# A place of its own for each row sum: the vector engine's scratch for row two moved into a freed transfer buffer

## Chip, cores, metric

One Trainium2 chip, one core. The time is microseconds (us) on the device for one launch, lower is better. The median of the kernel before is 82.82 us (82.77 to 82.85, 3 runs). Engines in short: PE (matmul), DVE (vector), ACT (scalar), POOL (GpSimd), SP (queues of transfers and the end).

## The reference, cut

```python
batch, num_classes = 256, 32000          # logits float32, 32.77 MB
log_probs = logits - max;  log_probs -= log(sum(exp(log_probs)))
smooth_targets = smoothing / num_classes everywhere, plus 1 - smoothing at the label
return -sum(smooth_targets * log_probs, axis=-1)      # one loss per row
```

Each logit is needed twice, in a sum of the logits and in a sum of their exps. The rest is work on one number per row.

## The kernel before, the parts that matter

128 partitions hold two rows each. A row is loaded in pieces; each piece goes to DVE (sum of the logits, by adding its two halves and accumulating) and to ACT (sum of exps). The pieces of row two get smaller so that little is left to do after the last has landed. The elementwise result of a sum is not needed, only its accumulator; it goes into a scratch, `jd`.

```python
WIDTHS = (
    (8000, 12480, 11520),
    (8576, 6400, 4608, 3392, 2496, 1856, 1408, 1088, 832, 704, 640),
)
FOLLOW = (1, 2, 6)   # row two's first 1 + 2 + 6 pieces reuse the three buffers wide0, wide1, wide2
# ... the last two pieces have buffers of their own (tail)

    def sum_logits(xt, w: int, out: bass.AP):
        h = w // 2
        jd = junk.tile([P, max(WIDTHS[0]) // 2], FP32, name="jd", tag="jd")   # bufs=1: one scratch
        return nc.vector.scalar_tensor_tensor(
            out=jd[:, :h], in0=xt[:, :h], scalar=1.0, in1=xt[:, h:w],
            op0=ALU.mult, op1=ALU.add, accum_out=out,
        )
# ...
    for t, w in enumerate(WIDTHS[r]):            # row two
        left = last - t
        xt = load(w, col)
        col += w
        part = sum_logits(
            xt, w, xsum[:, t + 1 : t + 2] if left > 1 else pairs[1 - left][:, 0:1]
        )
        # ... exps = sum_exps(...) on ACT; small additions on DVE when left <= 3
        elif left < 2:
            i = 1 - left
            nc.vector.tensor_tensor(out=done[i + 1][:], in0=done[i][:], in1=pairs[i][:], op=ALU.add)
# ... ln, two transposes, res, one store
```

As every sum writes the same scratch, a sum gets a wait for the sum ahead of it (a *self wait*: DVE waits on DVE), beside the wait for its transfer, unless an instruction between them has waited for that sum already. In the built program such a second wait stands in an instruction of its own ahead of the sum, which does nothing but wait (a *queue instruction*; DVEq in the chain).

The softmax here doesn't subtract the row's maximum and nothing guards it: scores larger than these inputs give would overflow.

## Time and profile before

| | before |
|---|---|
| median | 82.82 us |
| span of the profiled execution | 81.7 us |
| busy: DVE, ACT | 37.0 us (45%), 58.0 us (71%) |
| read from HBM (the chip's main memory) | 32.77 MB at 401 GB/s over the span |
| chain that ended last | transfers 81%, ACT 13%, DVE 2% |

The span is the time from the first to the last instruction in the profile. A transfer *lands* when its last byte has arrived. The chain is followed back from the last instruction, at each step to what released it. An engine's busy share says how much room it has; the chain and the waits say whether anything waits for it. The lines are in the prediction.

### The profile page before, as it was taken

The numbers are of one execution on the slowest core, as the hardware profiler recorded it, in microseconds if no ns is written. First come the engines' busy times: TensorE is split into PE (matmuls) and PEld (weight loads), VectorE is DVE, ScalarE is ACT, GpSimd is POOL, SyncE is SP. The second block draws the span as 40 slices with busy tenths as digits, with TensorE's granted clock in tenths as the row PEclk, the third lists the DMA queues.
The fourth block names the chain that finished last, engine by engine and source line by source line (L and its number), as shares of the span: only waits on it lengthen the run. The fifth ranks groups of instructions, "written<-read, shape, count | busy, mean of one in ns | idle before, by whom it ended". The sixth has DMA issues, their size and how long they took to land.

```text
span 81.7 us, 215 instructions
## 1 busy us (share of the span) xinstructions
PE 6.5 (8%) x21; PEld 4.6 (6%) x21; DVE 37.0 (45%) x37; ACT 58.0 (71%) x31; POOL 10.1 (12%) x19
## 2 busy tenths in 40 slices
PE   0000000000000000000000000000100000399302
PEld 0000000000000000000000000000000000378100
DVE  0000001990000899300299702990295748467772
ACT  5000001999200899993299998999999999999990
POOL 3201640040100000000000002991000000000000
PEclk9999999999999999999999999999999999999997
DMA  6999999999998888998699699999999999999910
GB/s 140 391 463 385 478 541 391 391 391 416 684 440 385 361 361 361 677 406 361 269 538 504 302 538 389 414 401 401 433 424 398 425 448 420 418 426 407 410 59 1
DMA packets 2258, 32.77 MB, mean 401 GB/s; under 512 B 337, under 2 KB 338, under 8 KB 1106
## 3 DMA queue, kind: packets, MB, share of 16 engines
q1 hardware_dynamic: 2018, 30.71, 88.6%
q10 hardware_dynamic: 144, 2.06, 5.9%
q0 software_dynamic: 96, 0.00, 0.1%
HBM read 32.77 MB, written 0.00 MB: 401 GB/s over the span
## 4 chain that ended last, share of the span: by engine, by line
DMA 81%; ACT 13%; DVE 2%; issue 1%; PE 0%; DVEq 0%
DMA wide<-in_logits_dram 57%; DMA tail<-in_logits_dram 24%; ACT ja L326 13%; DVE jd L311 1%; DVE done L421 0%; DVE lin_row L440 0%; PE lin_t L333 0%; DVE res L442 0%; DVEq L421 0%; DVEq L442 0%
## 5 line engine op out<-in xcount | busy, mean ns | idle before, releaser
L326 ACT ACTIVATE ja<-wide 128x8000 bf16<-128x8000 f32 (+4 forms) x5 | 40.2, 8033 | 20.8 <-DMA wide<-in_logits_dram 20.8
L311 DVE SCALAR_TENSOR_TENSOR jd<-wide 128x4000 f32<-128x4000 f32 (+11 forms) x12 | 34.5, 2876 | 39.0 <-DMA wide<-in_logits_dram 39.0
L326 ACT ACTIVATE jt<-wide 128x4608 bf16<-128x4608 f32 (+6 forms) x7 | 14.2, 2068 | 0.1
L428 PE MATMUL warm<-wide,ident 128*128 128x256 f32 x18 | 5.6, 479 | 12.0 <-DMA wide<-in_logits_dram 12.0
L428 PEld LDWEIGHTS warm<-wide,ident 128*128 128x128 f32 x18 | 4.4, 250 | 13.1 <-DMA wide<-in_logits_dram 12.3
L333 PE MATMUL loss_t<-ident,loss 128*1 128x128 f32 x1 | 0.4, 373 | 58.4 <-POOL loss L369 58.4
L358 POOL TENSOR_TENSOR lin<-acc,weighted 128x1 f32<-128x1 f32 x1 | 4.5, 4484 | 0.1
L333 PEld LDWEIGHTS loss_t<-ident,loss 128*1 128x1 f32 x1 | 0.1, 79 | 58.4 <-POOL loss L369 58.4
L353 POOL TENSOR_TENSOR acc<-sums 128x2 f32<-128x2 f32 x1 | 0.2, 192 | 16.2 <-ACT ja L326 16.2
L244 POOL DMA_INDIRECT gat<-in_logits_dram,flat_idx x2 | 2.0, 993 | 0.7 <-POOL ident masks.py:199 0.4
L372 DVE COPY res<-loss_t 1x128 f32<-1x128 f32 x1 | 0.3, 280 | 3.7 <-PE loss_t L333 3.7
L211 ACT ACT_TABLE_LOAD x1 | 1.3, 1283 | 0.9 <-PEq L469 0.9
L353 POOL TENSOR_TENSOR acc<-acc,sums 128x2 f32<-128x2 f32 x1 | 0.2, 193 | 12.6 <-ACT ja L326 12.6
L270 POOL TENSOR_SCALAR weighted<-gat 128x1 f32<-128x1 f32 x1 | 0.9, 867 | 6.4 <-DMA gat<-in_logits_dram,flat_idx 6.4
L326 ACT ACTIVATE jt<-tail 128x704 bf16<-128x704 f32 (+1 forms) x2 | 1.5, 764 | 0.0
L326 ACT ACTIVATION_READ_ACCUMULATOR jt<-wide 128x1 f32 x7 | 1.2, 166 | 0.0
L311 DVE SCALAR_TENSOR_TENSOR jd<-tail 128x352 f32<-128x352 f32 (+1 forms) x2 | 1.0, 510 | 0.1
L311 DVE DVE_READ_ACCUMULATOR jd<-wide 128x1 f32 x12 | 1.0, 82 | 0.0
L224 POOL DMA_DIRECT2D lab<-in_labels_dram x1 | 0.8, 766 | 1.0 <-POOLq L469 1.0
L326 ACT ACTIVATION_READ_ACCUMULATOR ja<-wide 128x1 f32 x5 | 0.9, 173 | 0.0
L236 POOL TENSOR_TENSOR flat_idx<-rowoff,lab 128x2 int32<-128x2 int32 x1 | 0.2, 193 | 5.3 <-DMA lab<-in_labels_dram 5.3
L270 POOL TENSOR_SCALAR xsum<-gat 128x1 f32<-128x1 f32 x1 | 0.2, 208 | 2.9 <-DMA gat<-in_logits_dram,flat_idx 2.9
(24 smaller groups left out, 4.7 us busy)
## 6 DMA issues: line engine op xcount, KB each, us to landing
wide<-in_logits_dram SPq DMA_DIRECT2D x1, 6240.0 KB, 25.9
wide<-in_logits_dram SPq DMA_DIRECT2D x1, 5760.0 KB, 39.1
wide<-in_logits_dram SPq DMA_DIRECT2D x1, 4288.0 KB, 29.6
wide<-in_logits_dram SPq DMA_DIRECT2D x1, 3200.0 KB, 20.5
wide<-in_logits_dram SPq DMA_DIRECT2D x1, 2304.0 KB, 25.8
wide<-in_logits_dram ACTq DMA_DIRECT2D x1, 2016.0 KB, 13.7
wide<-in_logits_dram SPq DMA_DIRECT2D x1, 1984.0 KB, 11.4
wide<-in_logits_dram SPq DMA_DIRECT2D x1, 1696.0 KB
```

The source lines that it names most:

```text
L211: nc.scalar.add_instruction(mybir.InstLoadActFuncSet(name=nc.get_next_instruction_name(), act_func_set_id=tbl, ins=[], outs=[],))
L224: nc.gpsimd.dma_start(out=lab[:], in_=labels.bitcast(I32).rearrange("(p f) -> p f", p=P))
L236: nc.gpsimd.tensor_tensor(out=flat_idx[:], in0=rowoff[:], in1=lab[:].rearrange("p (r two) -> p r two", two=2)[:, :, 0:1], op=ALU.add,)
L244: nc.gpsimd.indirect_dma_start(out=gat[:, r : r + 1], out_offset=None, in_=logits[:], in_offset=bass.IndirectOffsetOnAxis(ap=flat_idx[:, r ...
L270: nc.gpsimd.tensor_scalar(out=weighted[r], in0=gat[:, r : r + 1], scalar1=label_weight, scalar2=None, op0=ALU.mult,)
L311: return nc.vector.scalar_tensor_tensor(out=jd[:, :h], in0=xt[:, :h], scalar=1.0, in1=xt[:, h:w], op0=ALU.mult, op1=ALU.add, accum_out=out,)
L326: return nc.scalar.activation(out=ja[:, :w], in_=xt[:, :w], func=AF.Exp, accum_out=out)
L333: nc.tensor.transpose(out=row[:], in_=column, identity=ident[:])
L353: nc.gpsimd.tensor_tensor(out=acc[:], in0=total, in1=sums[:, :, t : t + 1], op=ALU.add)
L358: nc.gpsimd.tensor_tensor(out=lin[:], in0=total[:, 0, :], in1=weighted[0], op=ALU.add)
L372: nc.vector.tensor_copy(out=res[:, :, 0:1], in_=loss_t[:])
L428: nc.tensor.matmul(warm[:], lhsT=ident[:], rhs=xt[:, i * WARM_COLS : (i + 1) * WARM_COLS], start=True, stop=True,)
```

## The change

Intent: from the third piece of row two on (4608 columns), each sum gets a stretch of scratch of its own, so that no sum has to wait for the one ahead. That needs (4608 + 3392 + ... + 640) / 2 = 8512 columns, more than `jd` has. They are found in `wide0`, the buffer of row two's first piece, which no later load uses.

```diff
-    def sum_logits(xt, w: int, out: bass.AP):
+    SPARE_FROM = 2
+    spare_width = max(WIDTHS[0][0], WIDTHS[1][0])
+    spare = []
+    def sum_logits(xt, w: int, out: bass.AP, place: int | None = None):
         h = w // 2
-        jd = junk.tile([P, max(WIDTHS[0]) // 2], FP32, name="jd", tag="jd")
+        if place is None:
+            jd = junk.tile([P, max(WIDTHS[0]) // 2], FP32, name="jd", tag="jd")[:, :h]
+        else:
+            if not spare:
+                spare.append(wide.tile([P, spare_width], FP32, name="spare", tag="wide0"))
+            jd = spare[0][:, place : place + h]
         return nc.vector.scalar_tensor_tensor(
-            out=jd[:, :h],
+            out=jd,
# ... in row two's loop:
-            xt, w, xsum[:, t + 1 : t + 2] if left > 1 else pairs[1 - left][:, 0:1]
+            xt, w, xsum[:, t + 1 : t + 2] if left > 1 else pairs[1 - left][:, 0:1],
+            sum(WIDTHS[r][SPARE_FROM:t]) // 2 if t >= SPARE_FROM else None,
```

Seen in the built programs: the order of instructions is the same on all engines; six sums (3392 to 832 columns) lose their self wait; that of 4608 columns waits for ACT (end of the exp of the first piece) where it waited for DVE; the last two had no self wait before either, as the small additions ahead of them had already waited for it.

More of the change, by code (lines that the diff above doesn't have):

```diff
@@ L306, in load @@
         return xt
-    def sum_logits(xt, w: int, out: bass.AP):
-        h = w // 2
-        jd = junk.tile([P, max(WIDTHS[0]) // 2], FP32, name="jd", tag="jd")
+    SPARE_FROM = 2
+    spare_width = max(WIDTHS[0][0], WIDTHS[1][0])
+    assert FOLLOW[0] == 1 and sum(WIDTHS[1][SPARE_FROM:]) <= 2 * spare_width
+    spare = []
+    def sum_logits(xt, w: int, out: bass.AP, place: int | None = None):
+        h = w // 2
+        if place is None:
+            jd = junk.tile([P, max(WIDTHS[0]) // 2], FP32, name="jd", tag="jd")[:, :h]
+        else:
+            if not spare:
+                spare.append(
+                    wide.tile([P, spare_width], FP32, name="spare", tag="wide0")
+                )
+            jd = spare[0][:, place : place + h]
         return nc.vector.scalar_tensor_tensor(
-            out=jd[:, :h],
+            out=jd,
             in0=xt[:, :h],
@@ L390 @@
         part = sum_logits(
-            xt, w, xsum[:, t + 1 : t + 2] if left > 1 else pairs[1 - left][:, 0:1]
+            xt,
+            w,
+            xsum[:, t + 1 : t + 2] if left > 1 else pairs[1 - left][:, 0:1],
+            sum(WIDTHS[r][SPARE_FROM:t]) // 2 if t >= SPARE_FROM else None,
         )
```

## The prediction

> **What bounds the kernel now.** I read the page first (busy shares, then the chain that ended last), then the table of stages, then the instructions in order of time for the last 20 us, and last the waits. The chain:
>
> ```profile
> span 81.7 us, 215 instructions
> PE 6.5 (8%) x21; PEld 4.6 (6%) x21; DVE 37.0 (45%) x37; ACT 58.0 (71%) x31; POOL 10.1 (12%) x19
> DMA 81%; ACT 13%; DVE 2%; issue 1%; PE 0%; DVEq 0%
> HBM read 32.77 MB, written 0.00 MB: 401 GB/s over the span
> ```
>
> The reader is to see that the span is a transfer: 81% of the chain is the landing of logits, and the vector engine (DVE), which the change touches, holds 2%. Being busy 45% of the time says only that DVE has room. The 13% of ACT is one exp of the first row that holds a buffer which a later transfer needs; the change doesn't touch it. The stages of row two, from its first sum on (columns: stretch, its length, busy time and count of PE, PEld, DVE, ACT, POOL, then granted clock, DMA share, GB/s):
>
> ```profile
> 58.00:64.00 6.00, 0.37 (x1) 0.08 (x1) 3.93 (x4) 5.84 (x3) 0.19 (x1) 1.00 1.03 439
> 64.00:70.00 6.00, 0.00 (x0) 0.00 (x0) 4.26 (x4) 6.00 (x3) 0.00 (x0) 1.00 0.98 418
> 70.00:78.00 8.00, 5.59 (x18) 4.39 (x18) 5.23 (x15) 8.00 (x13) 0.00 (x0) 1.00 0.99 409
> 78.00:81.70 3.70, 0.54 (x2) 0.16 (x2) 1.82 (x8) 1.80 (x6) 0.00 (x0) 0.84 0.01 3
> ```
>
> Up to 78 us the DMA engines are full (0.98 to 1.03) and ACT is full too (6.00 of 6.00, 8.00 of 8.00), while DVE works 5.23 of 8. The widths were chosen so that each exp ends as the next piece lands. After 78 us nothing is transferred, and what remains is a serial end of 3.7 us. The changed sums, in order of time (start, duration, engine, what; in brackets the idle time before it and what ended it):
>
> ```profile
> 63.76 2.56 DVE L311 SCALAR_TENSOR_TENSOR jd<-wide 128x2304 f32<-128x2304 f32 x1 [1.27 <-DMA wide<-in_logits_dram]
> 67.76 1.93 DVE L311 SCALAR_TENSOR_TENSOR jd<-wide 128x1696 f32<-128x1696 f32 x1 [1.44 <-DMA wide<-in_logits_dram]
> ...
> 75.99 0.73 DVE L311 SCALAR_TENSOR_TENSOR jd<-wide 128x544 f32<-128x544 f32 x1 [0.39 <-DMA wide<-in_logits_dram]
> 77.00 0.59 DVE L311 SCALAR_TENSOR_TENSOR jd<-wide 128x416 f32<-128x416 f32 x1 [0.21 <-DMA wide<-in_logits_dram]
> ...
> 77.92 0.53 DVE L311 SCALAR_TENSOR_TENSOR jd<-tail 128x352 f32<-128x352 f32 x1
> 78.56 0.16 DVE L421 TENSOR_TENSOR done<-done,pair 128x2 f32<-128x2 f32 x1
> 78.71 0.49 DVE L311 SCALAR_TENSOR_TENSOR jd<-tail 128x320 f32<-128x320 f32 x1
> 79.32 0.16 DVE L421 TENSOR_TENSOR done<-done,pair 128x2 f32<-128x2 f32 x1
> ```
>
> Seven of the nine sums that move begin out of idleness, and what ends the idleness is always a piece landing. In all (columns: who waited for whom, us in total, times, longest):
>
> ```profile
> DVE jd L311 <- DMA wide<-in_logits_dram: 5.7, 7, 1.4
> ```
>
> The seven idle times are 1.27, 1.44, 1.04, 0.81, 0.56, 0.39 and 0.21 us, sum 5.7. No wait of a sum for an earlier sum shows in the view of waits at all.
>
> **What the Trainium skill says.** (1) "Perfetto Trace Analysis", Identifying Dependency Chains: an instruction that waits on several engines may get separate semaphore instructions ahead of it. The trace agrees: the chain has queue steps of DVE (DVEq, 0.02 us each) ahead of the small additions of line 421, which wait on DVE and ACT. The kernel sorts the waits so that the transfer's is taken by the sum itself. (2) "VectorE: DVE Perf Modes", The DRAIN you can't avoid: eight copies took the same 13.88 us with a semaphore behind each and with one behind the last. The trace agrees in part: the copy of line 404 begins at 76.64, within the sum that ends at 76.72; but where an addition must wait for a result, the chain has 0.09 us (0.03 issue, 0.02 DVEq, 0.04 issue) between them. (3) Same page, Two Vector instructions with no wait between them: a next instruction that is not held may start before the earlier one has finished. That is what freeing the sums from each other could in principle win; it needs two sums that stand back to back, and the trace shows none among those that lose a wait. (4) "SBUF — State Buffer", Who interferes with whom: transfers and engines use different ports, so a write of DVE into a transfer buffer should cost no more than one into other scratch. The trace agrees: see the fit below.
>
> **The change, part by part.** The order of instructions on all engines is the same before and after, with the same shapes: 14 sums, 14 exps, 15 loads. Only the waits of DVE differ.
>
> *Removed:* six sums (pieces of 3392, 2496, 1856, 1408, 1088 and 832 columns) wait for the earlier sum, since all write the same scratch, and for their transfer; afterwards they wait for the transfer alone. The wait taken away was over by the time of the transfer in each: the previous sum had ended 0.21 to 1.44 us earlier, except that the copy of line 404 stands between the last two. So each saves 0 on the path. If, against the trace, each cost its whole 0.09 us, the sum would be 6 x 0.09 = 0.54 us, 0.65% of 82.82: even the ceiling lies within 2%.
>
> *Replaced:* the sum of the 4608 piece waited for the previous sum (ended 62.49). It now waits for ACT's exp of the first piece of row two, the last reader of the buffer taken over. That exp and its accumulator read end at 57.75 + 0.15 = 57.90, the sum starts at 63.76: 5.86 us of slack. Cost 0.
>
> *Not changed:* the sums of the two last pieces (704 and 640) waited for their transfer alone before, and do so after; the additions of line 421 keep their waits. And these are the ones that set the end: the 704 piece lands at 77.90 and DVE goes on 0.02 later; then 0.55 + 0.09 + 0.16 + 0.50 + 0.10 + 0.17 us up to 79.49, then the transposes, the store. Nothing there loses a wait.
>
> *Buffers and transfers:* the scratch lies in the first transfer buffer after its second and last use. No load waits for it; the loads' waits are the same list. The first scratch keeps its size, so no address moves.
>
> *Duration of a sum:* from 128x320 in 0.494 us and 128x6240 in 6.657 us the slope is 6.163 / 5920 = 1.041 ns per element, the constant 0.161 us. The 128x2304 between them should then take 2.560, and took 2.559, with the DMA engines full. So no contention is there to be relieved, and I expect the same durations in the new place.
>
> Sum: 0 on the path; I allow 0.03 us for small shifts in the queue. 82.82 - 0.03 = 82.79, I say 82.8.
>
> **Rivals.**
> 1. *The self waits do cost.* If the engine's queue is slow to pick up a sum behind its separate wait, the sums start later after a landing than they could. Against it: DVE and ACT are released by the same landings and start together (63.76 and 63.76, 70.73 and 70.75), so DVE isn't the late one; and only the 832 piece's sum is close enough to the end to matter, since DVE is done with its batch (lines 410 and 407) at 77.87, 0.03 before the 704 piece lands. An earlier sum would then wait for that landing. At most 0.54 us: 82.3.
> 2. *A new wait on ACT.* ACT is the fuller engine, and the sum of 4608 now waits for it. For a cost, ACT would have to be 5.86 us later than now. If it were a wrong wait, for an exp later than that of the first piece, DVE would be tied to ACT, each sum behind an exp, perhaps 1 us more at the end: 83.8. The list of waits shows one wait only, on the sum of 4608.
> 3. *Writes into a transfer buffer meet the transfers.* In the last 15 us the transfers go into the neighbouring buffers at full rate. If a sum took 5% longer there, the two on the end's path would add 0.05 x (0.53 + 0.49) = 0.05 us: 82.9. If the batch before got longer than its 0.03 us of slack, some hundredths more.
> 4. *The time is the transfer's, and varies with it.* The profiled execution took 83.03 us, the median of three is 82.82. A difference of 0.2 us can come from the transfers alone, and would hide anything said above.
>
> **Range and chances.** The path gives 82.8. Rivals 1 and 3 move it by +0.1 or -0.3 in plausible sizes, and rival 4 by 0.2 either way, so 82.5 to 83.1 should hold 8 times in 10. Faster by 2% needs 81.2 us, three times the ceiling of rival 1; slower by 2% needs 84.5, which only rival 2 in a strong form comes near. Chances: 0.02 faster, 0.96 within 2%, 0.02 slower.
>
> **What would show it.** In the changed kernel's profile: the nine sums write the new scratch with durations within 0.02 us of those above; seven of them still begin out of idleness ended by a landing, total about 5.7 us; no wait on ACT for the 4608 sum; the chain from 77.9 us on has the same members and durations; DMA still some 81% of the chain and 401 GB/s. I am wrong if the sums' idle time falls while their starts move up against the exps released by the same landing (rival 1), if a wait of a sum on ACT appears (rival 2), if the sums lengthen (rival 3), or if the time after the last landing changes by more than 0.1 us. If only landings shift, with all else the same, it is rival 4.

## The result and the profile after

After: 82.87 us median (82.75 to 83.17, 6 runs), before in the same rounds 82.81 (82.74 to 83.17, 6 runs). Ratio 1.0004, 95% interval 0.9981 to 1.0027: the same. A ratio here is the mean time of one kernel's fast runs over that of the other's of the same rounds, so not quite the ratio of the medians; in the experiments below it fits the listed runs only if the first, profiled execution is left out.

From the page and the waits of the changed kernel: the span and the number of instructions, then who waited for whom (total us, times, longest).

```profile
span 81.6 us, 209 instructions
...
DVE spare L325 <- DMA wide<-in_logits_dram: 5.4, 7, 1.4
```

There were 215 instructions before: the six that are missing are the separate queue instructions that carried the six self waits. So the change did what it was to do. But the nine sums in the new place still begin, seven times, only when a piece lands, and idle 5.4 us for it (5.7 before). The same sums in order of time:

```profile
63.65 2.56 DVE L325 SCALAR_TENSOR_TENSOR spare<-wide 128x2304 f32<-128x2304 f32 x1 [1.02 <-DMA wide<-in_logits_dram]
...
67.66 1.93 DVE L325 SCALAR_TENSOR_TENSOR spare<-wide 128x1696 f32<-128x1696 f32 x1 [1.44 <-DMA wide<-in_logits_dram]
...
75.87 0.73 DVE L325 SCALAR_TENSOR_TENSOR spare<-wide 128x544 f32<-128x544 f32 x1 [0.38 <-DMA wide<-in_logits_dram]
...
76.89 0.59 DVE L325 SCALAR_TENSOR_TENSOR spare<-wide 128x416 f32<-128x416 f32 x1 [0.21 <-DMA wide<-in_logits_dram]
...
77.80 0.53 DVE L325 SCALAR_TENSOR_TENSOR spare<-tail 128x352 f32<-128x352 f32 x1
...
78.58 0.49 DVE L325 SCALAR_TENSOR_TENSOR spare<-tail 128x320 f32<-128x320 f32 x1
```

Durations are those of before to 0.01 us and idle times to 0.02 us, but for the first idle time (1.02 for 1.27). There the sum ahead ended 0.14 us later (62.63 for 62.49) and the piece of 4608 landed 0.11 us earlier. That is not the change: two kernels below that keep this sum's self wait (each sum twice, waits kept; written over the piece before) show 1.03 and 1.01 us there. From the start of the 352-element sum to that of the last DVE instruction (`res`) it is 77.80 to 80.09 = 2.29 us, before 77.92 to 80.22 = 2.30. The pieces landed 0.1 us earlier in this execution, and the sums and the end moved with them, no more.

One view looks quite different, the chain's shares by engine; here of the changed kernel:

```profile
DMA 57%; ACT 23%; issue 16%; PE 0%; DVE 0%
```

Before it was DMA 81%, ACT 13%. The change did not cause this: the same changed kernel, profiled once more (first experiment), has the old chain again.

```profile
DMA 81%; ACT 13%; DVE 2%; issue 1%; PE 0%; DVEq 0%
```

The reason stands at the end. The last DVE instruction waits for two things, DVE's own copy `lin_row` and PE's transpose `lse_t` of ACT's result. In the changed kernel's timeline:

```profile
79.71 0.28 DVE L457 COPY lin_row<-lin_t 1x128 f32<-1x128 f32 x1 [0.36 <-PE lin_t L347]
...
79.78 0.27 PE L347 MATMUL lse_t<-ident,lse 128*1 128x128 f32 x1
80.09 0.28 DVE L459 SCALAR_TENSOR_TENSOR res<-lin_row,lse_t 1x128 f32<-1x128 f32 x1
```

They end at 79.99 and 80.05. From the end of `lin_row` to `res` the chain of before has 0.09 us (0.03 issue, 0.02 DVEq, 0.04 issue), from the end of `lse_t` that of the changed kernel has 0.04, so the two sides reach `res` within some 0.01 us of each other. In before they do as well: `lin_row` ends at 80.12, `lse_t` at 80.16, and `res` starts at 80.22. Whichever side is later by a hundredth decides whether the chain is followed back through DVE to the last landing, or through ACT's row of exps, which in turn keep pace with the landings. The page splits a tie at its end into two very different pies.

### The profile page after: what moved, and what is told of

Read it like the earlier page. It is cut to its first block, busy times and chain, and to the rows that moved or that the text cites. A ratio compares the mean times of both kernels' runs of the same rounds, so it can differ in the third digit from the quotient of the medians.

```text
span 81.6 us, 209 instructions
## 1 busy us (share of the span) xinstructions
PE 7.7 (9%) x21; PEld 5.4 (7%) x21; DVE 37.0 (45%) x37; ACT 57.8 (71%) x31; POOL 10.2 (12%) x19
## 4 chain that ended last, share of the span: by engine, by line
DMA 57%; ACT 23%; issue 16%; PE 0%; DVE 0%
DMA wide<-in_logits_dram 57%; ACT ja L340 20%; ACT jt L340 3%; PE lse_t L347 0%; DVE res L459 0%; ACT lse L454 0%
## 5 line engine op out<-in xcount | busy, mean ns | idle before, releaser
L325 DVE SCALAR_TENSOR_TENSOR jd<-wide 128x4000 f32<-128x4000 f32 (+4 forms) x5 | 25.2, 5047 | 33.5 <-DMA wide<-in_logits_dram 33.5
L325 DVE SCALAR_TENSOR_TENSOR spare<-wide 128x2304 f32<-128x2304 f32 (+6 forms) x7 | 9.3, 1326 | 5.4 <-DMA wide<-in_logits_dram 5.4
L445 PE MATMUL warm<-wide,ident 128*128 128x256 f32 x18 | 6.8, 560 | 11.7 <-DMA wide<-in_logits_dram 11.7
L445 PEld LDWEIGHTS warm<-wide,ident 128*128 128x128 f32 x18 | 5.2, 295 | 13.2 <-DMA wide<-in_logits_dram 12.0
L325 DVE SCALAR_TENSOR_TENSOR spare<-tail 128x352 f32<-128x352 f32 (+1 forms) x2 | 1.0, 508 | 0.0
L325 DVE DVE_READ_ACCUMULATOR spare<-wide 128x1 f32 x7 | 0.6, 83 | 0.0
```

Of the source, the lines that this page charges most:

```text
L325: return nc.vector.scalar_tensor_tensor(out=jd, in0=xt[:, :h], scalar=1.0, in1=xt[:, h:w], op0=ALU.mult, op1=ALU.add, accum_out=out,)
L445: nc.tensor.matmul(warm[:], lhsT=ident[:], rhs=xt[:, i * WARM_COLS : (i + 1) * WARM_COLS], start=True, stop=True,)
```

## The experiments

My theory: a self wait is over before the landing that releases the sum, so taking it away wins nothing, and nothing on DVE before the 704 piece has landed can win anything. Rivals: (a) the two halves of the change cancel, a gain from the waits and a loss from the new place; (b) the sums do hold something back, and the change only failed to free it; (c) self waits cost nothing anywhere. Each experiment's times are beside runs of the kernel before on the same chip; the first four shared one chip (before 82.78 us median, 11 runs), the next three another (82.81, 9 runs), the last three ran together, on the chip of the first four. Their runs of before (82.77, 12 runs) are the 11 of the first four, some 12 minutes older, and one more.

**The changed kernel again.**

> The changed kernel once more, on the chip of the next three, so that small differences have a common yardstick. Theory (the waits taken away were over before the landing that released each sum): ratio to before 1.000, within 0.003. Rival 'the waits cost and the new place costs as much, so they cancel here': the same here; the next two runs tell them apart.

82.80 us, ratio 1.0000 (0.9987 to 1.0012). With this the difference is known to be under 0.15 us either way.

**Own places, but inside the old scratch** (one half of the change):

```diff
-    SPARE_FROM = 2
-    spare_width = max(WIDTHS[0][0], WIDTHS[1][0])
+    SPARE_FROM = 3
+    spare_width = max(WIDTHS[0]) // 2
-                    wide.tile([P, spare_width], FP32, name="spare", tag="wide0")
+                    junk.tile([P, spare_width], FP32, name="spare", tag="jd")
```

> A place of its own for each sum from the piece of 3392 on, but inside the old scratch: five self waits fewer, nothing written into a transfer buffer. Theory: ratio to before within 0.003 of 1, sums' idle times and durations as before. Rival 'cancelling': waits cost about 0.09 us each, so this half alone gains 0.3 to 0.5 us, ratio 0.994 to 0.996.

82.82 us, ratio 1.0006 (0.9994 to 1.0018); 210 instructions, so five waits fewer. No gain from the waits alone.

**The freed buffer, but one place** (the other half):

```diff
-            sum(WIDTHS[r][SPARE_FROM:t]) // 2 if t >= SPARE_FROM else None,
+            0 if t >= SPARE_FROM else None,
```

> The scratch in the freed transfer buffer, but one place for all sums, so the six self waits stay: the other half alone. Theory: ratio within 0.003 of 1 and durations of the nine sums within 0.02 us of before (0.49 to 2.56). Rival 'cancelling': this half alone loses 0.3 to 0.5 us, ratio 1.004 to 1.006, and its sums are longer.

82.91 us, ratio 1.0006 (0.9993 to 1.0020; with the profiled execution of 83.28 us it would be 1.0015); 215 instructions; the nine sums take 0.49 to 2.56 us as before. No loss of the size that the rival asked for (1.004 to 1.006). Rival (a) is out: there is nothing to cancel.

**No middle sums at all** (a wrong result; those sums enter the loss with a factor of 0.1/32000):

```diff
+    nc.gpsimd.memset(xsum[:], 0.0)
-        part = sum_logits(xt, w, ...)
+        if t < 2 or left < 2:
+            part = sum_logits(xt, w, ...)
```

> Wrong result on purpose: the kernel before without the seven sums of the pieces 4608 to 832, with xsum set to zero in their place. It takes away all that the change touches, but for the two last sums. Theory (the landings set the pace up to 77.9 us): ratio 1.000 within 0.003. Rival 'the sums hold something back (engine, memory or transfers), and the change failed to free it': a gain, 0.5 us or more.

82.82 us, ratio 1.0004 (0.9992 to 1.0016). Seven sums with 9.3 us of busy time are gone, and the time is the same. This is the strongest bound: whatever one does to these seven sums, nothing can be won beyond the noise (0.07 us, by the interval). The timeline shows why: DVE now idles until the 704 piece lands, and starts its sum at 77.89 (77.92 before), in both 0.02 us after the landing.

```profile
77.89 0.53 DVE L312 SCALAR_TENSOR_TENSOR jd<-tail 128x352 f32<-128x352 f32 x1 [0.52 <-DMA tail<-in_logits_dram]
```

Rival (b) is out. Do self waits cost anything, then? For that DVE has to be the late one.

**Each sum twice, waits kept** (before's kernel; from the piece of 3392 on, the second result in a spare column):

```diff
+        if t >= 3:
+            part = sum_logits(xt, w, extra[:, t : t + 1])
```

> The kernel before with each sum from the piece of 3392 on done twice (the second into a spare column), all in the one scratch: 16 sums back to back, each waiting for the one ahead, so DVE falls behind the landings and sets the end. Both theories: slower than before. Worked out from before's durations: 2 x 7.75 us of sums, 16 gaps of 0.09, 0.5 for the additions between, from 67.8 us on: DVE ends at 85.2 in place of 79.5, time about 88.5 us.

**Each sum twice, all in places of their own** (changed kernel with SPARE_FROM = 3, and the second sums in `jd` at the same offsets):

```diff
+            if second and not again:
+                again.append(junk.tile([P, max(WIDTHS[0]) // 2], FP32, name="again", tag="jd"))
+            jd = (again if second else spare)[0][:, place : place + h]
```

> The same 16 sums, but each in a place of its own (first ones in the freed buffer, second ones in the old scratch): one self wait left among the sums. My theory (a self wait costs where sums stand back to back: 0.09 us of gap and about 0.08 us of overlap lost, and nothing where a landing comes later): about 86.4 us, some 2 us under the waiting one, and sums start before the one ahead ends. Rival 'a self wait costs nothing even back to back[...]': within 0.3 us of the waiting one.

87.93 us with waits (ratio 1.0617, 1.0600 to 1.0634), 85.91 without (1.0375, 1.0360 to 1.0391): 2.02 us apart, where I had said some 2. Both came 0.5 us under my figures. In the waiting one the sums began at 67.66 and not 67.8, and from there to the end of the last addition (84.37) the gaps and additions came to 1.26 us beside 15.45 of sums, where I had allowed 1.94; the end after it took 3.56 us, not 3.3. The built programs differ by 12 waits of DVE on itself (16 on sums, against one on a sum, one on the reduction and two on additions). The two sums of 928 elements and the sum that follows, with waits:

```profile
74.73 1.12 DVE L311 SCALAR_TENSOR_TENSOR jd<-wide 128x928 f32<-128x928 f32 x1
75.78 0.08 DVE L311 DVE_READ_ACCUMULATOR jd<-wide 128x1 f32 x1
75.90 1.12 DVE L311 SCALAR_TENSOR_TENSOR jd<-wide 128x928 f32<-128x928 f32 x1
76.95 0.08 DVE L311 DVE_READ_ACCUMULATOR jd<-wide 128x1 f32 x1
77.14 0.89 DVE L311 SCALAR_TENSOR_TENSOR jd<-wide 128x704 f32<-128x704 f32 x1
```

and without:

```profile
74.11 1.12 DVE L329 SCALAR_TENSOR_TENSOR spare<-wide 128x928 f32<-128x928 f32 x1
75.15 0.08 DVE L329 DVE_READ_ACCUMULATOR spare<-wide 128x1 f32 x1
75.15 1.12 DVE L329 SCALAR_TENSOR_TENSOR again<-wide 128x928 f32<-128x928 f32 x1
76.20 0.09 DVE L329 DVE_READ_ACCUMULATOR again<-wide 128x1 f32 x1
76.20 0.89 DVE L329 SCALAR_TENSOR_TENSOR spare<-wide 128x704 f32<-128x704 f32 x1
```

Start to start, the first pair takes 75.90 - 74.73 = 1.17 us with the wait and 1.04 without: the wait costs 0.13. To the next sum, which waits for a transfer as well, it is 1.24 against 1.05: 0.19. There the self wait stands in a queue instruction of its own; though the piece had landed long before (the exp of that piece ran from 74.6), the extra instruction costs. Over the pieces 3392 to 1408 the two costs are 0.11 to 0.13 and 0.19 to 0.20. Without a wait the next sum starts together with the accumulator read of the one ahead, 0.08 to 0.09 us before that ends. One thing else differs in the built programs: where nobody waits for them, 9 of the 16 sums don't signal their end any more. It is not what counts, as the last sums (of 832, 704 and 640 columns) signal in both and overlap just the same without a wait (the two of 352 elements start 0.44 us apart, at a duration of 0.52). Rival (c) is out: the change takes away a real cost, from a place where nobody pays it.

**A wait that is not hidden.** The kernel before, with the sums from 3392 on (1856 excepted, because PE still reads the piece before it) written over the piece before, so that each waits for ACT's exp of that piece (*tied* to it, below):

```diff
-    def sum_logits(xt, w: int, out: bass.AP):
+    def sum_logits(xt, w: int, out: bass.AP, into=None):
+        jd = into
+        if into is None:
+            jd = junk.tile(...)
# in row two's loop, with before = xt of the previous turn:
+            before if t >= 3 and left != WARM_LEFT - 1 else None,
```

> The kernel before, but the sums from the piece of 3392 on (that of 1856 excepted) are written over the piece before, so each waits for ACT's exp of that piece, which ends as late as the landing or later. A wait that is not hidden. Theory: at the end the sum of 704 columns starts at the end of the exp of 832 (78.08 + 0.05) and not at 77.92, that of 640 at 78.84 + 0.05 and not at 78.71: +0.2 us, ratio 1.002 to 1.003. Rival 'only landings and their spread count, what DVE waits for changes nothing visible': the traces' sums start as before and the end after the last landing is as long.

83.44 us, ratio 1.0078 (1.0065 to 1.0092): 0.65 us, three times what I had said. The spans, 81.74 on average against 81.49 before, give 0.25 us, the size that the theory has, though not by its way: in the trace the sum of 704 starts at 78.10, behind the reduction ahead of it (77.92 to 78.08), while the exp's accumulator read was over at 78.00. The late sum of 832 had pushed the reduction. The sums' durations are as before (0.49 to 1.93), so it is the waits that cost, not the place. The other 0.4 us lies outside the span of the profile: time minus span is 1.73 us on average, against 1.32 for before, and 1.31 to 1.36 for each of the six experiments above. Three more runs were to place that.

**The same again, then its halves.** Only the last two sums tied (`before if left < 2`), and only the middle ones (`before if t >= 3 and left >= 2 and left != WARM_LEFT - 1`):

> The same kernel as the one written over the piece before, which cost 0.65 us where I had said 0.2: its spans were 0.25 us longer, as said, but the time outside the span was 1.7 us in place of 1.3. Is that outside part the kernel's? If it is an accident of that chip or session, this run has 1.3 us outside and a ratio of 1.003; if the kernel's, 1.7 us and 1.008 again.

> Only the two last sums (704 and 640 columns) are written over the piece before and wait for ACT's exp. In the span: the sum of 704 starts about 0.25 us after its landing in place of 0.02, the span is 0.15 to 0.25 us longer. Outside the span: 1.7 us if what costs there comes from these two, 1.3 if from the middle ones.

> Only the sums of 3392 to 832 columns (that of 1856 excepted) are tied to the exp before, the two last are as before. In the span: the sum of 832 starts about 0.25 us after its landing, so DVE ends the small additions after the 704 piece has landed and not 0.03 us before: 0.15 to 0.2 us longer. Outside: 1.7 us if the middle ones cost there, 1.3 if not.

| | time | ratio (95%) | mean span, longer than before by | time minus span |
|---|---|---|---|---|
| before | 82.77 | | (its span: 81.47) | 1.33 |
| all tied, again | 83.46 | 1.0086 (1.0071 to 1.0101) | 0.28 | 1.73 |
| last two tied | 83.00 | 1.0025 (1.0010 to 1.0039) | 0.21 | 1.33 |
| middle ones tied | 83.32 | 1.0067 (1.0051 to 1.0084) | 0.16 | 1.72 |

Spans are on record to 0.1 us each, so the differences of their means are good to some hundredths only. Inside the span the theory's sizes hold: 0.21 us for the last two (said 0.15 to 0.25), 0.16 for the middle ones (said 0.15 to 0.2). The last two tied is the clean case, as nothing is lost outside. Its timeline:

```profile
77.69 0.21 ACT L328 ACTIVATION_READ_ACCUMULATOR jt<-wide 128x1 f32 x1
77.79 0.79 ACT L328 ACTIVATE jt<-tail 128x704 bf16<-128x704 f32 x1
78.00 0.52 DVE L313 SCALAR_TENSOR_TENSOR wide<-tail 128x352 f32<-128x352 f32 x1 [0.32 <-ACT jt L328]
...
80.21 0.28 DVE L446 SCALAR_TENSOR_TENSOR res<-lin_row,lse_t 1x128 f32<-1x128 f32 x1
```

and of before:

```profile
77.96 0.79 ACT L326 ACTIVATE jt<-tail 128x704 bf16<-128x704 f32 x1
...
80.22 0.28 DVE L442 SCALAR_TENSOR_TENSOR res<-lin_row,lse_t 1x128 f32<-1x128 f32 x1
```

DVE was free at 77.68 and waits for ACT's accumulator read, which ends at 77.90; before, it waited for nothing but the landing. From the start of ACT's exp of that piece (77.79 here, 77.96 before) to `res` (80.21, before 80.22) it is 2.42 us for 2.26. So a wait costs something here from the last two sums on, or where it eats the 0.03 us of slack ahead of them (the middle ones).

The 0.4 us outside the span belongs to the kernel with the middle sums tied, three times out of three (1.73, 1.73 and 1.72), on two chips, while the last two tied, run in the same rounds, had 1.33. What it is stays open: the profile's first and last instructions are as before, and the built programs' opening and closing instructions are the same. It doesn't touch the change studied here, which had 1.30 us outside.

No version beat both kernels, and with the middle sums worth nothing there was none to try among them.

## Why the prediction was right

82.8 us was said, 82.87 measured, inside 82.5 to 83.1, and the ratio says no change. By its steps:

- *Six self waits removed, 0 on the path.* Right: 215 to 209 instructions, idle times before the sums unchanged but for the first (explained above), and the waits alone (own places in the old scratch, five of the six) gave 1.0006.
- *One wait replaced by one on ACT, 0.* Right: in the list of waits of the profile no sum waits for ACT.
- *Same durations in the new place.* Right, to 0.01 us, and shown by itself (freed buffer, one place: 1.0006).
- *The end is not touched.* Right: 2.29 us for 2.30.
- *The ceiling of 0.54 us if each wait cost 0.09 in full.* Too low. The 0.09 counted the gap behind an addition that must wait. The overlap lost and the extra queue instruction come on top: 0.19 us each, measured back to back, so 6 x 0.19 = 1.1 us, 1.4% of the time. The conclusion (within 2% even then) stood, with less room than I claimed. Reading (2) of the skill was too kind, too: that the copy of line 404 starts within the sum ahead speaks against a semaphore that costs nothing, and the sums done twice showed the cost.
- *Rival 1*, that self waits slow the pick-up behind a landing: refuted here, though they do cost where sums queue. *Rival 2*, a wait on ACT: refuted, and its size known now: had the sums really been tied to the exps, it would have been 0.25 us inside the span and 0.65 to 0.7 us in all, the rest outside and unexplained, not the 1 us I gave it. *Rival 3*: refuted (the first seven sums took what they took before while the transfers ran at 407 to 436 GB/s). *Rival 4*, spread of the transfers: this is what is left of the differences; the unchanged kernel ranged over 82.69 to 83.17.
- *The 0.03 us allowed for shifts in the queue* was a guess that no run resolves; that 82.8 lay 0.07 us from the median is within the spread and proves nothing by itself.
- *The marker "the chain from 77.9 us on has the same members, DMA some 81%"* was a bad one: it failed in the first profile of the changed kernel and held in the second. The end is a tie of ACT and DVE, and the chain takes one side of it.

## What to carry to other kernels

A wait is worth removing only where it ends last. Look at what ended the idle time before each instruction: if it is a landing, the other waits of that instruction cost nothing (six here), and deleting the whole instruction, with a wrong result, bounds what any change to it can win in one run. Where instructions queue back to back on DVE, on the other hand, separate scratch for each is worth 0.11 to 0.20 us per instruction here. Don't take a change of the chain's shares for a change of the kernel before looking for a tie at its end.

## What the Trainium skill lacked or had wrong

- "VectorE: DVE Perf Modes", The DRAIN you can't avoid, has it that a semaphore between chained operations costs nothing extra (measured there on eight copies) and that the next one doesn't start before the pipe is empty, though it sends the reader on for a next one that is not held. Here sums of 128x704 to 128x1696 back to back lost 0.11 to 0.13 us each to a self wait, and 0.19 to 0.20 where the sum waits for a transfer too; without the wait they started 0.08 to 0.09 us before the accumulator read ahead had ended. The same page's section on two instructions with no wait between them fits these runs better, and gives no figure for what it is worth.
- "Perfetto Trace Analysis", Identifying Dependency Chains, says that several waits may become extra semaphore instructions, but not what one costs: some 0.07 us here where nothing hides it (0.19 to 0.20 against 0.11 to 0.13 us), nothing where a landing comes later.
- No page that I found says that a change in a kernel's middle alone can cost time outside the profiled span (it would belong in "Runtime: NRT & Kernel Launch"): 0.4 us here with the middle sums tied to ACT (1.72 and 1.73 against 1.33 us), cause open.
